# Quarter products for queries, keys and six gates in three interleaved sets

## Chip, cores and metric

The kernel runs on one core of a Trainium2 chip. The metric is device time in microseconds of one launch; the median of three runs is given. The core has TensorE (PE; matmuls, with weight loads shown apart as PEld), VectorE (DVE), ScalarE (ACT), GpSimd (POOL) and SyncE (SP, which here issues the DMAs). Each engine works through its own instructions in order and waits for the others by semaphores.

## The reference, cut to what matters

One decoder layer over 512 positions of width 1024, in float32. After a norm, one large projection `u @ w_in` gives queries, keys and values of three attention groups (six heads of 64 each), the input of a pooling branch, the z, xBC and dt inputs of a state-space (SSD) branch, and three gates of width 1024. Each branch ends in a projection to width 1024, which is multiplied by the sigmoid of its gate; the three are added, projected, and a gated ConvFFN follows.

```python
proj = u @ w_in[i]
q, k, v, pool_in, z, xbc, dt_raw, gate_pre = jnp.split(proj, split_idx, axis=-1)
g = jax.nn.sigmoid(gate_pre + b_gate[i])          # three gates, 1024 wide each
...
o, lse = dilated_group_attention(q[:, :, hs], k[:, :, hs], v[:, :, hs], rel_bias[:, hs], dilation, window // dilation)
xbc = jax.nn.silu(causal_dwconv(xbc, conv_w, conv_b))   # four taps, 1536 channels
```

What matters here: group 1 of the attention needs 384 columns of queries and 384 of keys; the gate of the second branch (pooling) has eight blocks of 128 columns; xBC has twelve.

## The kernel before

**Split precision.** Every large product is three matmul passes over rounded parts: high times high, high times low, low times high (`mm3`). The activations are kept as `uh` and `ul`. Weights are fetched by DMA into `raw`, rounded on ACT into `wh` (`cast`, line 195), and DVE makes the rest, `wl = raw - wh` (`lows`, line 215). `mm3` uses `wl` in the last third of its matmuls.

**Jobs and order.** `program()` yields the weight jobs in order. The main loop goes through them: before the body of job n, `prepare` writes the low part of n+1 and then `then` of n+1 (a sum on weights), puts the cast of n+2 on the list `second`, and fetches n+3. The casts have two halves. `flush()` takes what is on the list: it is called at the beginning of each `step()`, and the main loop calls it before the next job until the list is empty. The first half's call puts the second half on the list. The instructions of PE, ACT, DVE and POOL stay in the order in which the program writes them (`ORDERED`); SP's order is left to the scheduler.

**Side work.** `step()` is called within job bodies. It moves on all generators in `running` and starts one item of `waiting`. An attention item of `attend(g)` writes scores on PE (for every second head), then bias add and maximum on DVE, four exponentials on ACT; two steps later it turns the probabilities on PE, copies them out, and pairs of heads go on to the output product.

**A gate or xBC block** is a "column": 24 matmuls 512 wide into one bank, then an evacuation (gate: sigmoid on ACT, product on DVE; xBC: one ACT instruction, three on DVE) and a `step()`. A job of 256 columns holds two.

**Seven quarter products.** For a pair of blocks (left and right) the product over the even and odd blocks of the contraction and the halves of the positions is made as seven products of a quarter instead of eight. Their sums of activations are made once (`sums_of_u`), their sums of weights on DVE for each set (line 339). `v_pair` does so for the values of groups 1 and 2 (384 columns each; positions as the stationary side), `qk_sevens(1)` for queries and keys of group 1 (384 columns each; 36 matmuls 256 wide for each of seven products). The other products stay whole.

**PSUM** has four banks with tag "mm" (`MM`) and four with tag "sm" (`SM`). Attention items and other side work take "sm" banks, whole products "mm" banks. The raw weights have two buffers, `wh` three, `wl` two, and `ypool` two: these hold the two weight quarters `w` of a set of sevens, later the xBC blocks 0 to 7.

**Order around the change:** second branch's projection, value pair's weights, gates 0 to 3 (`SPLIT` is 4), seven value products, four products of queries and keys, gates 4 and 5, one product, gates 6 and 7, two products, `attend(1)`, twelve xBC columns, `ssd_start`, queries and keys of group 2.

Of the kernel before, what the change touches and what calls it, by code (L numbers as in the profile page):

```python
# [83 lines left out]
def trunk(ctx: ExitStack, tc, out, x, rel_bias, ln1_g, w_in, b_gate, w_a, pool_w, pool_scale, w_b,  # L84
# [235 lines left out]
    def sums_of(f0, f1, ah, al, found):  # L320
# [3 lines left out]
        dve.tensor_tensor(sa[:, LO], f0[:, HI], f1[:, HI], OP.add)  # L324
        dve.tensor_tensor(sa[:, HI], sa[:, LO], f0[:, LO], OP.subtract)
        dve.tensor_tensor(sb[:, LO], f0[:, LO], f0[:, HI], OP.subtract)
        dve.tensor_tensor(sb[:, HI], f1[:, LO], sa[:, HI], OP.subtract)
# [14 lines left out]
    def sevens(quarter, c, side, W, emit):  # L342

        r1, r2, r3, r5 = {}, {}, {}, {}

        def job(j, load, form, use):
            def body(ws):
                wh, wl = ws  # L350
                parts = side(j)
                for i in range(2):
                    ps = MM("pb")
                    o = slice(i * P, (i + 1) * P)
                    mm3(ps[:, :c], lambda k: wh[:, k, :], lambda k: wl[:, k, :],
                        lambda k: parts[k][0][:, o], lambda k: parts[k][1][:, o], range(4), flip=True)
                    use(i, ps[:, :c])
                step()
            new = Job([load] if load is not None else [], 4, c, body)
            new.form = form  # L360
            if load is None:
                new.load = lambda: None
            return new

        def keep(r, name):
            def use(i, ps):
                r[i] = T(name)[:, :c]
                act.copy(r[i], ps)
            return use

        def p5(i, ps):
            keep(r5, "r5")(i, ps)
            dve.tensor_tensor(r2[i], r2[i], ps, OP.add)

        def p6(i, ps):
            dve.tensor_tensor(r1[i], r1[i], ps, OP.add)
            emit(0, 1, i, r1[i], r2[i])

        def p7(i, ps):
            r3[i] = T("r3")[:, :c]  # L380
            dve.tensor_tensor(r3[i], r1[i], ps, OP.add)
            emit(1, 1, i, r3[i], r5[i])

        one = job("A11", quarter(0, 0), None, keep(r1, "r1"))
        two = job("A12", quarter(1, 0), None, lambda i, ps: emit(0, 0, i, r1[i], ps))
        three = job(4, None, lambda: W[1], keep(r2, "r2"))
        one.then = lambda: diff(one.raw, W[0], one.raw)
        three.then = lambda: diff(W[0], W[1], W[0])
# [1367 lines left out]
```

## Time and profile before

| | |
|---|---|
| runs | 1035.77, 1034.72, 1035.15 us (median 1035.15) |
| profiled execution | 1034.7 us, of which 1033.0 us span from first to last instruction |
| TensorE busy | 1022.2 us, mean granted clock 0.998 |
| DVE, ACT, POOL busy | 690.9, 473.3, 149.6 us |
| the changed stretch | about 190 to 371 us of the span |

A row of the groups' view reads: line, engine, operation, out<-in, shapes, count, then total busy us, mean ns of one, then idle time of the engine before them and what ended it. A row of the timeline: start, length in us, engine, line, operation, and in brackets the idle time before it and who ended it. A row of the chain in order of time: start, length, what.

### The profile page before, as it was taken

Reading aid. Unit: us, or ns where it says so; the run is one execution under the profiler, and the core shown is the slowest. Engines: PE = TensorE matmul, PEld = TensorE weight load, DVE = VectorE, ACT = ScalarE, POOL = GpSimd, SP = SyncE. Lnnn points to the kernel's source line nnn. Section 1 sums busy time; section 2 is a strip of 40 time slices with the busy share of each in tenths; the row PEclk is TensorE's granted clock in tenths of the full one; section 3 lists DMA queues with packets and bytes.
Section 4 is the critical chain, followed back from the end, with each engine's and each line's share of the span. In section 5 each row is a group of like instructions: output and inputs, shape, how many; then the busy total and the mean of one; then the engine's idle time right before and its main releaser. Section 6 shows DMA issues by size and latency. Waiting matters only on the chain.

```text
span 1033.0 us, 13348 instructions
## 1 busy us (share of the span) xinstructions
PE 1022.2 (99%) x5312; PEld 863.1 (84%) x5312; DVE 690.9 (67%) x921; ACT 473.3 (46%) x779; POOL 149.6 (14%) x125
## 2 busy tenths in 40 slices
PE   9999999999999999999999999999999999999997
PEld 9998878899888878888888888898888888888885
DVE  5553566687567658766768656766768676666775
ACT  6432554453356364557445324545444443453342
POOL 2770000000000004210152501101111001111120
PEclk9999999999999999999999999999999999999999
DMA  8344312035242244452244525543233324323142
GB/s 289 115 129 138 109 54 75 31 102 172 94 139 84 86 127 116 144 140 67 67 148 152 174 82 204 171 141 121 82 102 124 102 82 163 123 81 122 62 143 82
DMA packets 115997, 122.35 MB, mean 118 GB/s; under 512 B 5315, under 2 KB 98310, under 8 KB 115935
## 3 DMA queue, kind: packets, MB, share of 16 engines
q1 hardware_dynamic: 115343, 120.64, 36.7%
q8 instruction: 42, 0.69, 0.3%
q10 hardware_dynamic: 592, 0.86, 0.3%
q14 instruction: 20, 0.16, 0.1%
HBM read 117.69 MB, written 2.22 MB: 116 GB/s over the span
## 4 chain that ended last, share of the span: by engine, by line
PE 93%; DVE 3%; ACT 2%; DMA 1%; issue 1%; ACTq 0%; SPq 0%; DVEq 0%
PE pa L234 35%; PE pu L234 21%; PE pb L234 10%; PE p L234 10%; PE pqk L234 6%; PE pa L1607 2%; PE ps L751 1%; PE pu L1407 1%; DVE wl L215 1%; PE ppw L234 1%; PE pt L779 1%; PE po L792 1%; PE py L1077 1%; ACT wh L195 1%; DMA xin<-in_x_dram 1%; PE pyo L1084 1%
## 5 line engine op out<-in xcount | busy, mean ns | idle before, releaser
L215 DVE TENSOR_TENSOR wl<-raw,wh 128x2048 fp32r<-128x2048 f32 (+3 forms) x96 | 218.5, 2278 | 46.7 <-ACT wh L195 38.8
L195 ACT CAST wh<-raw 128x1024 fp32r<-128x1024 f32 (+3 forms) x190 | 189.9, 1017 | 54.9 <-DVE raw L339 32.3
L1268 DVE SCALAR_TENSOR_TENSOR hc<-pu,fcol,hc 128x510 f32<-128x510 f32 x88 | 65.8, 748 | 61.0 <-ACT hc L1265 59.4
L234 PE MATMUL pa<-uh,wh 128*128 128x512 f32 x384 | 98.6, 399 | 0.0
L234 PE MATMUL pa<-ul,wh 128*128 128x512 f32 x384 | 94.9, 389 | 0.0
L234 PE MATMUL pa<-uh,wl 128*128 128x512 f32 x384 | 94.9, 389 | 0.0
L234 PEld LDWEIGHTS pa<-ul,wh 128*128 128x128 f32 x384 | 72.1, 188 | 15.2
L234 PEld LDWEIGHTS pa<-uh,wl 128*128 128x128 f32 x384 | 72.1, 188 | 14.9
L234 PE MATMUL pu<-uh,wl 128*128 128x512 f32 (+1 forms) x352 | 83.6, 380 | 0.2 <-DVE wl L215 0.2
L234 PE MATMUL pu<-uh,wh 128*128 128x512 f32 (+1 forms) x352 | 83.6, 379 | 0.0
L234 PE MATMUL pu<-ul,wh 128*128 128x512 f32 (+1 forms) x352 | 83.5, 379 | 0.0
L234 PEld LDWEIGHTS pa<-uh,wh 128*128 128x128 f32 x384 | 70.1, 188 | 14.5 <-issue 0.7
L234 PEld LDWEIGHTS pu<-uh,wl 128*128 128x128 f32 x352 | 64.1, 188 | 13.0 <-DVE wl L215 0.6
L234 PEld LDWEIGHTS pu<-ul,wh 128*128 128x128 f32 x352 | 64.2, 188 | 12.5
L234 PEld LDWEIGHTS pu<-uh,wh 128*128 128x128 f32 x352 | 64.1, 188 | 12.4
L1273 POOL TENSOR_TENSOR hc<-hc 128x512 f32<-128x512 f32 x22 | 30.4, 1383 | 279.2 <-DVE hc L1268 244.2
L1265 ACT ACTIVATE hc<-pu,fcol,fcol 128x512 f32<-128x512 f32 x40 | 31.2, 780 | 82.0 <-PE pu L234 81.7
L1039 POOL TENSOR_TENSOR xd<-xc,dec 128x512 f32<-128x512 f32 x6 | 6.4, 1063 | 331.5 <-DVE xc L1033 312.6
L772 ACT ACTIVATE sb<-sb,both 128x128 f32<-128x128 f32 (+1 forms) x72 | 30.1, 419 | 33.2 <-DVE both L769 23.2
L1166 ACT ACTIVATE sg<-pa,col 128x512 f32<-128x512 f32 x24 | 16.5, 688 | 58.1 <-PE pa L234 51.3
L1270 ACT ACTIVATE hc<-hc 128x512 f32<-128x512 f32 x22 | 13.9, 632 | 42.9 <-DVE hc L1268 42.9
L915 DVE SCALAR_TENSOR_TENSOR xs<-pa,col,xs 128x509 f32<-128x509 f32 (+2 forms) x24 | 18.0, 749 | 16.4 <-ACT xs L911 15.8
(377 smaller groups left out, 1863.1 us busy)
## 6 DMA issues: line engine op xcount, KB each, us to landing
raw<-in_w_in_dram SPq DMA_DIRECT2D x25, 1024.0 KB
raw<-in_ffn_w_up_dram SPq DMA_DIRECT2D x22, 1024.0 KB
raw<-in_ffn_w_down_dram SPq DMA_DIRECT2D x11, 1024.0 KB
raw<-in_w_o_dram SPq DMA_DIRECT2D x8, 1024.0 KB
raw<-in_w_in_dram SPq DMA_DIRECT2D x14, 512.0 KB
raw<-in_w_in_dram SPq DMA_DIRECT2D x8, 768.0 KB
raw<-in_w_b_dram SPq DMA_DIRECT2D x4, 1024.0 KB
al<-ad SPq DMA_DIRECT2D x16, 256.0 KB
```

Of the source, the lines that this page charges most:

```text
L195: act.copy(job.high[:, :, o], job.raw[:, :, o])
L215: (eng or dve).tensor_tensor(l[:, :, o], job.raw[:, :, o], h[:, :, o].bitcast(F32), OP.subtract)
L234: pe.matmul(ps, l, r, start=first and n == 0, stop=last and n == total - 1, skip_group_check=again)
L751: pe.matmul(pss[i][:, o:o + w * P], q[r, n * P:(n + 1) * P], k[r, kb * P:(kb + w) * P], start=True, stop=True)
L772: act.activation(sb[:, off:off + w * P], sb[:, off:off + w * P], AF.Exp, bias=nm[:, n, h:h + 1], accum_out=ls[:, n, h:h + 1])
L915: dve.scalar_tensor_tensor(t[:, sh:], ps[:, :S - sh], col[:, o_cw + 12 * k + m:o_cw + 12 * k + m + 1], t[:, sh:], OP.mult, OP.add)
L1166: act.activation(s, ps, AF.Sigmoid, bias=col[:, o:o + 1])
L1265: act.activation(t, ps, AF.Identity, bias=ff["c1"][:, ff["b"] + m:ff["b"] + m + 1], scale=fw(2, m))
L1268: dve.scalar_tensor_tensor(t[:, sh:], ps[:, :S - sh], fw(k, m), t[:, sh:], OP.mult, OP.add)
L1270: act.activation(t, t, AF.Silu)
L1273: pool.tensor_tensor(a, a, t, OP.mult)
L1607: pe.matmul(first[2 * n + j][:, lo:hi], a[:, k, j * P:(j + 1) * P], b[:, k, lo:hi], start=a is wh and b is uh and k == 0, stop=a is wl and ...
```

## The change

The sets of seven are built by one function, `sevens`, whose weight sums are additions in place on the two held quarters (`plus`); the activation sums change sign to match. `v_pair` keeps its sums in PSUM: one, six, seven and four add up in the same banks X, five and three in Z, and two in Y; X and Z are "sm" banks. In place of `qk_sevens` there are three sets of two blocks on each side (256 columns): Q0 Q1 with K0 K1, Q2 G0 with K2 G1, G2 G3 with G4 G5, where G are gates of the second branch. Each of a set's seven products has 24 matmuls 256 wide, in four "mm" banks held across the three sets. A step follows every second product.

The order changes too: xBC columns 8 and 9 and gates 6 and 7 come ahead of the value products; the 21 products of the sets are interleaved; xBC columns 10 and 11 stand as single columns (jobs of 128 columns, one step) ahead of the last set's seven and four; `attend(1)` is called after the second set's four, with five products and the two single columns still to come; xBC columns 0 to 7 follow.

```diff
@@ -317,14 +317,14 @@
-    def sums_of(f0, f1, ah, al, found):
+    def sums_of(f0, f1, ah, al, found, s=1):
-        dve.tensor_tensor(sa[:, LO], f0[:, HI], f1[:, HI], OP.add)
+        dve.tensor_tensor(sa[:, LO], f0[:, HI], f1[:, HI], OP.add if s > 0 else OP.subtract)
-        dve.tensor_tensor(sb[:, HI], f1[:, LO], sa[:, HI], OP.subtract)
+        dve.tensor_tensor(sb[:, HI], f1[:, LO], sa[:, HI], OP.subtract if s > 0 else OP.add)
...
-    def sevens(quarter, c, side, W, emit):
...
+    SIDES = {"one": "A11", "two": "A12", "three": 4, "four": "A22", "five": 1, "six": 2, "seven": 3}
+
+    def sevens(quarter, c, W, body):
+
+        jobs = {}
+
+        def plus(to, what):
+            dve.tensor_tensor(to, to, what, OP.add)
+
+        def put(name, source=None, w=0):
+            job = jobs[name] = Job(source or [], 4, c,
+                                   lambda ws: body(name, ws, side_u(SIDES[name])))
+            if source is None:
+                job.load = lambda: None
+                job.form = lambda: W[w]
+
+        for name in ("one", "five", "six", "four"):
+            put(name)
+        put("seven", w=1)
+        put("two", quarter(1, 0))
+        put("three", quarter(1, 1))
+
+        def both_():
+            plus(W[0], jobs["three"].raw)
+            plus(W[1], jobs["three"].raw)
+
+        jobs["one"].then = lambda: plus(W[0], W[1])
+        jobs["three"].then = both_
+        jobs["six"].then = lambda: plus(W[0], jobs["two"].raw)
+        return jobs
...
-                           lambda j, h, l: US.__setitem__((j, p), (h, l)))
+                           lambda j, h, l: US.__setitem__((j, p), (h, l)), -1)
...
+        X, Y, Z, r1, r5 = {}, {}, {}, {}, {}
+        banks = {"one": X, "six": X, "seven": X, "four": X, "five": Z, "three": Z, "two": Y}
...
+        def use(name, i, ps):
+            if name == "one":
+                r1[i] = copy(ps, "r1")
+            elif name == "five":
+                r5[i] = copy(ps, "r5")
+            elif name != "three":
+                t, send = out(name in ("seven", "four"), name in ("six", "seven"), i)
+                if name == "two":
+                    dve.tensor_tensor(t, ps, r1[i], OP.add)
+                elif name == "six":
+                    dve.tensor_tensor(t, Z[i][:, :384], copy(ps, "r2"), OP.subtract)
+                elif name == "seven":
+                    dve.tensor_tensor(t, r5[i], copy(ps, "r7"), OP.subtract)
+                else:
+                    act.copy(t, ps)
+                send()
+
+        def body(name, ws, parts):
+            wh, wl = ws
+            bank = banks[name]
+            if name == "one":
+                for i in range(2):
+                    Z[i] = SM("p5")
+                for i in range(2):
+                    X[i] = SM("p1")
+            fresh = name in ("one", "two", "five")
+            for i in range(2):
+                if name == "two":
+                    Y[i] = MM("p2")
+                ps = bank[i][:, :384]
+                o = slice(i * P, (i + 1) * P)
+                mm3(ps, lambda k: wh[:, k, :], lambda k: wl[:, k, :],
+                    lambda k: parts[k][0][:, o], lambda k: parts[k][1][:, o], range(4),
+                    fresh, True, flip=True, again=not fresh)
+                use(name, i, ps)
+            step()
+
+        jobs = sevens(lambda two, h: [quarter(two, h)], 384, W, body)
+        return load, [jobs[n] for n in ("one", "five", "two", "three", "six", "seven", "four")]
 
     def qk_jobs(g):
...
-    def qk_sevens(g):
...
+    def q_sink(g, c):
+        t = QK["q", g, c] = T(f"q{g}")
+        half = lambda hi: grouped(t, g)[:, :, 64 * hi:64 * hi + 64]
+
+        def two(ps, r):
+            dve.scalar_tensor_tensor(half(0), turned_(ps), 0.125, turned_(r), OP.mult, OP.add)
+
...
+    ROLE, turn_of = {}, [0]
+
+    def set_of_sevens(lefts, rights, x, scales=(1.0, 1.0)):
...
+        def bank(which):
+            if not ROLE:
+                for n in ("c", "y", "a", "b"):
+                    ROLE[n] = MM("p")
+            return ROLE[which]
...
+        def use(name, ps):
+            if name in ("two", "six"):
+                for j, (_, make) in enumerate(lefts if name == "two" else rights):
+                    sinks[name == "six", j] = make()
+            if name == "one":
+                copy(ps, "one", scales)
+            elif name == "five":
+                copy(ps, "five")
+            elif name == "two":
+                for j in range(2):
+                    sinks[0, j][0](cut(ps, j), cut(r["one"], j))
+            elif name == "six":
+                t = copy(ps, "r2")
+                for j in range(2):
+                    sinks[1, j](0, cut(bank("b"), j), cut(t, j))
+            elif name == "seven":
+                t = copy(ps, "r7")
+                for j in range(2):
+                    sinks[1, j](1, cut(r["five"], j), cut(t, j))
+            elif name == "four":
+                for j in range(2):
+                    sinks[0, j][1](cut(ps, j))
+
+        def body(name, ws, parts):
+            wh, wl = ws
+            ps = bank(role.get(name, x))
+            fresh = name in ("one", "two", "five")
+            for c in range(2):
+                cs = slice(c * P, (c + 1) * P)
+                mm3(cut(ps, c), lambda k: wh[:, k, cs], lambda k: wl[:, k, cs],
+                    lambda k: parts[k][0], lambda k: parts[k][1], range(4),
+                    fresh and c == 0, True, again=not fresh or c == 1)
+            use(name, ps)
+            turn_of[0] += 1
+            if turn_of[0] % 2 == 0:
+                step()
+
+        return load, sevens(lambda two, h: [src for _, _, src in quarter(two, h)], 256, W, body)
 
     def attend(g):
...
+    def gate_sink(b, m, left):
+        t = T("gr")
+
+        def gate(to, ps):
+            o = o_bg + 8 * b + m
+            act.activation(to, ps, AF.Sigmoid, bias=col[:, o:o + 1])
+
+        def times():
+            dve.tensor_tensor(MG[m], MG[m], t, OP.mult)
+
+        def two(ps, r):
+            dve.tensor_tensor(t[:, LO], ps, r, OP.add)
+            gate(t[:, LO], t[:, LO])
+
+        def four(ps):
+            gate(t[:, HI], ps)
+            times()
+
+        def put(hi, x, y):
+            dve.tensor_tensor(t[:, (LO, HI)[hi]], x, y, OP.subtract)
+            if hi:
+                gate(t, t)
+                times()
+
+        return (two, four) if left else put
+
     def gate_jobs(b, lo=0, hi=8):
         def evac(m, ps):
...
         load, pair = v_pair()
+        Q = lambda i: (C_Q + 384 + i * P, lambda: q_sink(1, i))
+        K = lambda i: (C_K + 384 + i * P, lambda: k_sink(1, i))
+        G = lambda i, left: (C_GATE + D + i * P, lambda: gate_sink(1, i, left))
+        BC = lambda lo, hi, width: jobs_a(w_in, C_XBC + lo * P, hi - lo, uhk, ulk, KD,
+                                          lambda m, ps: xbc_evac(lo + m, ps), width)
+        loads, s = zip(
+            set_of_sevens((Q(0), Q(1)), (K(0), K(1)), "a", (0.125, 0.125)),
+            set_of_sevens((Q(2), G(0, True)), (K(2), G(1, False)), "c", (0.125, 1.0)),
+            set_of_sevens((G(2, True), G(3, True)), (G(4, False), G(5, False)), "a"))
         yield Call(load)
-        yield from gate_jobs(1, 0, SPLIT)
-        load, begun, ended = qk_sevens(1)
+        yield from BC(8, 10, 256)
+        yield from gate_jobs(1, 6, 8)
         for i, job in enumerate(pair):
             yield job
-            if i == 5:
-                yield Call(load)
-        yield from begun
-        yield from gate_jobs(1, SPLIT, SPLIT + 2)
-        yield ended[0]
-        yield from gate_jobs(1, SPLIT + 2)
-        yield from ended[1:]
-        yield Call(lambda: attend(1))
-        yield from jobs_a(w_in, C_XBC, 12, uhk, ulk, KD, xbc_evac)
+            if i in (4, 5):
+                yield Call(loads[i - 4])
+        spare = BC(10, 12, P)
+        for i, n in ((0, "one"), (0, "five"), (0, "two"), (0, "three"), (0, "six"), (1, "one"),
+                     (0, "seven"), (1, "five"), (0, "four"), (1, "three"), (1, "two"), (1, "six"),
+                     (2, "one"), (1, "seven"), (2, "five"), (1, "four"), (2, "three"), (2, "two"),
+                     (2, "six"), (2, "seven"), (2, "four")):
+            if (i, n) == (0, "four"):
+                yield Call(loads[2])
+            if (i, n) in ((2, "seven"), (2, "four")):
+                yield next(spare)
+            yield s[i][n]
+            if (i, n) == (1, "four"):
+                yield Call(lambda: attend(1))
+        yield from BC(0, 8, 256)
         yield Call(ssd_start)
         yield from qk_jobs(2)
         yield Call(lambda: attend(2))

```

172 lines of the change are left out of this document (50 added, 122 removed).

## The prediction

> **What bounds the kernel now.** I read the page first (busy shares, clock), then TensorE's waits, then the stretch the change touches by windows, by the chain in order of time and by queue.
>
> ```profile
> span 1033.0 us, 13348 instructions
> PE 1022.2 (99%) x5312; PEld 863.1 (84%) x5312; DVE 690.9 (67%) x921; ACT 473.3 (46%) x779; POOL 149.6 (14%) x125
> ...
> PEclk9999999999999999999999999999999999999999
> ```
>
> ```profile
> PE p L234 <- DVE wl L215: 0.5, 1, 0.5
> ```
>
> In the second fence the columns are waiter, releaser, total, times, longest. TensorE is busy 1022.2 of 1033.0 us at full clock. So two things count: matmul time removed, and every microsecond in which TensorE is made to wait, because nothing behind it has slack to give that back. In the stretch of the change it waits once today, 0.5 us for a low part (wl). The profiled execution took 1034.7 us (span 1033.0 and 1.7 around it); the median of the runs is 1035.15, 0.45 more. I sum against 1034.7 and add 0.45 at the end. About 0.2% (2.1 us) can be told from no change.
>
> **Matmul time.** The chain in order of time gives both rates.
>
> ```profile
> 253.48 10.91 PE pa L234 x48
> 264.39 4.31 PE p L234 x36
> ```
>
> A gate's matmul 512 wide costs 10.91/48 = 0.227 us, a 256-wide one of a quarter product 4.31/36 = 0.120 us: two of these are 0.240, so splitting loses 5% of a column's price. Before, six gates are 6x24 = 144 wide ones (32.7 us), queries and keys 7x36 = 252 narrow ones (30.2 us). After, three sets of seven products of 24 are 504 narrow ones: 60.3 us. Seven eighths of the gates' work would be 4.1 us less; the narrower form leaves **-2.6 us**. The value pair keeps its 168 matmuls. The old wait of 0.5 us belongs to the handover from the pair to the old products and goes: **-0.5**.
>
> **What the vector and scalar engines get.** A set's product lasts 24x0.120 = 2.9 us (the old: 4.3). Its weights must pass ACT (cast, two halves), then DVE (low part).
>
> ```profile
> L215 DVE TENSOR_TENSOR wl<-raw,wh 128x2048 fp32r<-128x2048 f32 x10 | 22.9, 2286 | 5.7 <-ACT wh L195 5.7
> L195 ACT CAST wh<-raw 128x1024 fp32r<-128x1024 f32 x20 | 20.8, 1042 | 6.2 <-DMA raw<-in_w_in_dram 6.2
> L215 DVE TENSOR_TENSOR wl<-raw,wh 128x1536 fp32r<-128x1536 f32 x7 | 12.3, 1756 | 1.9 <-ACT wh L195 1.8
> L195 ACT CAST wh<-raw 128x768 fp32r<-128x768 f32 x14 | 11.2, 833 | 6.4 <-DVE raw L339 6.2 <-DMA raw<-in_w_in_dram 0.2
> ...
> L339 DVE TENSOR_TENSOR w<-w,w 128x1536 f32<-128x1536 f32 x2 | 3.5, 1754 | 0.0
> ...
> L1168 DVE TENSOR_TENSOR yo<-yo,sg 128x512 f32<-128x512 f32 x5 | 3.5, 690 | 13.4 <-ACT sg L1166 13.4
> L1166 ACT ACTIVATE sg<-pa,col 128x512 f32<-128x512 f32 x5 | 3.5, 690 | 16.3 <-PE pa L234 16.3
> ...
> L707 DVE TENSOR_TENSOR k<-p,r 128x256 f32<-128x256 f32 x3 | 1.8, 615 | 0.2 <-ACT r L706 0.2
> ```
>
> ```profile
> L1176 ACT COPY yo<-pa x8: 582/586/589, 128.5 to 182.0; 128x512 f32<-128x512 f32 x8
> ```
>
> ```profile
> L324 DVE TENSOR_TENSOR sa<-uf x4: 410/415/418, 175.7 to 198.1; 128x256 f32<-128x256 f32 x4
> ```
>
> The tile views give least, median and most. Drawn on to the new sizes, a cast half of 512 elements is 0.62 us, a low part or a plus of 1024 elements 1.23 (by the step from 1536 to 2048). Per set DVE has 7 lows and 4 pluses, 13.5 us, and its evacuations: six of 0.6 for queries and keys (3.6), or for set 2, all gates, six sums of 0.42 and four products of 0.69 (5.3). That is 17 to 19 of 20.1 us: the mean fits. The old pair loses eight value adds on DVE and gains four copies on ACT; xBC columns 8 and 9 and gates 6 and 7 ahead of it put 2x(3x0.75-0.69) = 3.1 us more on DVE beside 21.8 us of matmuls, in-place sums and the reordered banks add nothing there, DMA carries 1.5 MB less of weights: all **zero**, covered by the matmuls; without that cover the 3.1 us would count.
>
> What isn't covered is the order. A cast for the product after next stands on ACT behind the evacuation of the present one, and the low on DVE behind that. From a product's end to its successor's successor there is 2.9 us and, as wl is first used after 8 matmuls, 0.96 more: 3.8 us. Followed through the queues with these durations:
> - Set 0, six: three ends only one product ahead, and its low (1.23) and two pluses (2.5) stand on DVE before the two query sums (1.2) and the low of six. 0.2 + 0.6 + 1.15 + 1.23 + 2.5 + 1.2 + 1.23, less 0.4 that back-to-back instructions overlap, is 7.7 us after two began; the matmuls get there in 6.7: **0.9** lost.
> - Set 1, four: behind seven's copy 0.6, key difference 0.6, gate difference 0.42, sigmoid 0.69, cast 1.15, low 1.23 with handovers 0.3, 5.0 against 3.8: **1.1**. Three more places lose 0.2 to 0.3 (pair's six, set 2's one, set 1's seven): **0.7**.
>
> These 2.7 us could be 0 if all of it ran ahead, or twice that if the sums on one weight tile wait for each other; I take 2.7.
>
> **Attention among the last products.** attend(1) is now called after set 1's four, so its first four items fall on the steps of set 2's two, the first single xBC column, set 2's seven and the second single column. Before, they fell on whole xBC columns. One such step today, on ACT, then on DVE, and a step's scores and transposes on TensorE:
>
> ```profile
> 293.75 0.78 ACT L911 ACTIVATE xs<-pa,col 128x512 f32<-128x512 f32 x1 [3.56 <-PE pa L234]
> 294.43 1.04 ACT L195 CAST wh<-raw 128x1024 fp32r<-128x1024 f32 x1
> 295.48 1.28 ACT L772 ACT_TABLE_LOAD   x1
> 298.23 0.40 ACT L772 ACTIVATE sb<-sb,both 128x128 f32<-128x128 f32 x1 [1.47 <-DVE both L769]
> ...
> 299.69 0.19 ACT L772 ACTIVATION_READ_ACCUMULATOR sb<-sb,both 128x1 f32 x1
> 300.51 0.78 ACT L911 ACTIVATE xs<-pa,col 128x512 f32<-128x512 f32 x1 [0.63 <-PE pa L234]
> 301.19 1.04 ACT L195 CAST wh<-raw 128x1024 fp32r<-128x1024 f32 x1
> ```
>
> ```profile
> 294.56 2.31 DVE L915 SCALAR_TENSOR_TENSOR xs<-pa,col,xs 128x509 f32<-128x509 f32 x3 [2.04 <-ACT xs L911]
> 296.79 0.68 DVE L765 TENSOR_TENSOR sb<-ps,b 128x512 f32<-128x512 f32 x1
> 297.51 0.69 DVE L769 TENSOR_REDUCE both<-sb 128x4 f32<-128x512 f32 x1
> ```
>
> ```profile
> 305.91 1.09 PE ps L751 x16
> 307.00 0.58 PE pt L779 x4
> ```
>
> The reader should see that from the column's end (293.7) to the last exponential (299.8) ACT's queue is held 6.1 us, and that a job's two cast halves stand on either side of it: the first before the exponentials, the second after. Today the second has another 5.5 us column for cover. In the change a single column or a product has one step, so the second half comes behind the exponentials, and the cover is a 2.9 us product:
> - First single column: the item's scores (1.09) end, add and maximum 1.4, exponentials 1.65, half 0.62: 5.1 after two's end, against 1.09 + 2.9 of matmuls, and some 0.2 of handovers: **1.3**.
> - Second single column: 6.1 + 0.6 after the first, against product 2.9, scores 1.09, transposes 0.58, plus handovers: **2.4**.
> - Set 2's four: from the second column's start DVE has its low 1.23, seven's two gates in turn with ACT (0.42 + 0.69 + 0.69, twice), add and maximum 1.4, then exponentials 1.65, half 0.62, low 1.23: 9.7; the matmuls reach the first wl in 5.45 + 0.58 + 0.96 = 7.0: **2.7**.
> - First whole xBC column: by the order of allocation its bank is the one that four has just filled, and four's two sigmoids stand on ACT behind the second column's 0.7 + 2.31 on DVE, add and maximum, exponentials, a copy 0.56, a cast half 1.04 and a table change 1.28. From four's low to the bank's release 8.5 us, of which four's rest of 16 matmuls covers 1.9: **6.6**. With another bank only wl is late: 3.4.
>
> Sigmoids and exponentials now alternate: five table changes for one today. Most fall into waits; the one before four's gates doesn't, and is priced above by its row.
>
> ```profile
> 364.53 1.04 ACT L195 CAST wh<-raw 128x1024 fp32r<-128x1024 f32 x1
> 365.59 1.28 ACT L1096 ACT_TABLE_LOAD   x1
> 366.88 1.16 ACT L1096 ACTIVATE xcv<-xcv 128x512 f32<-128x512 f32 x2
> ```
>
> Here the load starts as the cast ends and the next activation starts as the load ends: 1.28 us in all. [...]
>
> The sum: -2.6 - 0.5 + 2.7 + (1.3 + 2.4 + 2.7 + 6.6 = 13.0) = **+12.6 us**, 1047.3 for the profiled execution, **1047.8** on the scale of the median. The same with the cheaper bank and small product waits: 1042; with doubled ones: 1051.
>
> **The rivals.**
> 1. *Faster.* ACT and DVE run a product ahead all through, so no cast or low is late, and only -3.1 is left: 1032.1. It decides when all new waits together stay below 1.0 us.
>
> ```profile
> 279.60:288.30 8.70, 8.70 (x74) 8.67 (x73) 6.57 (x6) 5.27 (x10) 0.00 (x0) 1.00 0.39 122
> ```
>
> For it: in this window (stretch, length, then busy time and count of PE, PEld, DVE, ACT, POOL) two old products keep TensorE busy throughout, with DVE at 76%. Against: such a job lasts 4.3 us and takes two steps. Chance 0.13.
> 2. *About the same.* The second cast halves get ahead of the exponentials, so the 13.0 shrinks to 1.6 (four's low and bank without attention, 0.5 + 1.1): -3.1 + 2.7 + 1.6 = +1.2, 1036.3. The three ACT rows 294.43 to 301.19 speak against it: order is kept. Chance 0.10.
> 3. *Late weights.* The pair's value rows go out by SP.
>
> ```profile
> 235.94 10.54 SPq L624 DMA_DIRECT2D vr<-v  x16
> 246.59 46.33 SPq L183 DMA_DIRECT2D raw<-in_w_in_dram  x8
> ```
>
> ```profile
> 251.72 2.00 ACT L195 CAST wh<-raw 128x1024 fp32r<-128x1024 f32 x2 [5.73 <-DMA raw<-in_w_in_dram]
> ```
>
> If two's weights of set 0 stand behind sixteen sends (10.5 us) and land 5.1 us after issue, two starts up to 6.9 us late: up to 1054.7. For it: at 251.72 ACT waited 5.73 us for exactly that. Against: its slot is free long before. Chance 0.07.
> 4. *Slower clock.* [...] Chance 0.06. [...]
>
> That the change saves no matmuls can be left out: the counts are in the code.
>
> **How the numbers follow.** The forecast has 0.64. Faster by over 0.2% is rival 1: 0.13; within 0.2% rival 2: 0.10; slower the rest, 0.77. The range leaves out rival 1 and the end of rival 3: 1036 to 1053.
>
> **What would show it.** In the changed profile: 5420 matmuls, TensorE's busy time of narrow matmuls 60 us, five table loads between the first set and the second whole xBC column, TensorE's waits led by ACT (gr, the first whole column's bank) and by wh and wl around the single columns, 10 to 17 us in all, and no wait downstream changed. It is wrong if these waits add to under 5 us, or if exponentials come behind both halves of a cast.

## The result: 1046.4 us against 1035.3, slower by 1.1%, and the profile after

The changed kernel takes 1046.42 us (median; 1045.84 to 1047.41), the kernel before 1035.3 (four runs now, 1034.72 to 1035.77); the ratio is 1.0109 with an interval of 1.0091 to 1.0126. The prediction said 1047.8. Sign, size and place are as predicted. Inside the sum the terms at attention were too large, and a wait that was to go came back in the same place; that the total comes so close is in part luck.

The page of the changed kernel, in the parts that answer to those shown of before:

```profile
span 1044.1 us, 13664 instructions
...
PE 1024.6 (98%) x5420; PEld 868.4 (83%) x5420; DVE 703.5 (67%) x942; ACT 490.1 (47%) x815; POOL 148.9 (14%) x125
```

TensorE has 2.4 us more of busy time and, with the longer span, 8.7 us more of idle. The matmuls are fewer in work but more in number (5420). Its waits (waiter, releaser: total, times, longest):

```profile
PE pa L234 <- ACT wh L195: 3.4, 2, 2.2
PE pa L234 <- DVE wl L215: 3.1, 1, 3.1
PE p L234 <- DVE wl L215: 2.9, 4, 1.1
PE pa L1648 <- DVE relb L497: 1.1, 1, 1.1
PE pcb L1051 <- ACT xcv L1139: 1.0, 1, 1.0
```

The last two rows stood in before as well. The first three are new: 9.4 us, of which 6.5 lie at whole columns (pa) and 2.9 at quarter products (p). Before there was one such row, 0.5 us. By windows, the stretch falls apart as follows (stretch, length, busy time and count of PE, PEld, DVE, ACT, POOL, then TensorE's granted clock, DMA share, GB/s):

```profile
206.30:235.80 29.50, 29.45 (x169) 29.10 (x168) 21.80 (x20) 14.74 (x24) 0.00 (x0) 1.00 0.32 99
235.80:291.40 55.60, 53.55 (x433) 52.15 (x432) 42.73 (x44) 27.73 (x54) 0.00 (x0) 1.00 0.34 100
291.40:331.00 39.60, 31.90 (x197) 26.81 (x198) 23.15 (x32) 26.32 (x60) 0.00 (x0) 0.96 0.26 79
```

The pair (first row) is nearly gapless. 18 quarter products (second row) idle 2.1 us. The stretch with attention and the two single columns (third row) idles 7.7 us of 39.6, and its clock is 0.96. TensorE's own rows there show each place, with the idle time and its cause in brackets:

```profile
240.32 0.74 PE L234 MATMUL p<-sah,wl 128*128 128x256 f32 x4 [0.53 <-DVE wl L215]
249.94 0.74 PE L234 MATMUL p<-sah,wl 128*128 128x256 f32 x4 [0.72 <-DVE wl L215]
283.55 0.74 PE L234 MATMUL p<-uh,wl 128*128 128x256 f32 x4 [0.56 <-DVE wl L215]
296.91 2.11 PE L234 MATMUL pa<-uh,wh 128*128 128x512 f32 x8 [1.27 <-ACT wh L195]
309.37 3.51 PE L234 MATMUL pa<-uh,wh 128*128 128x512 f32 x8 [2.18 <-ACT wh L195]
319.22 0.74 PE L234 MATMUL p<-uh,wl 128*128 128x256 f32 x4 [1.12 <-DVE wl L215]
321.24 2.00 PE L234 MATMUL pa<-uh,wh 128*128 128x512 f32 x8
328.19 2.14 PE L234 MATMUL pa<-uh,wl 128*128 128x512 f32 x8 [3.14 <-DVE wl L215]
```

In order: set 0's five, set 0's six, set 1's four, the first single column, the second single column, set 2's four, and the first whole column, which starts without a wait at 321.24 and then stands 3.14 us at its low part. ACT's rows before the second single column give the reason, the same as in the prediction's rows of before:

```profile
303.36 0.61 ACT L195 CAST wh<-raw 128x512 fp32r<-128x512 f32 x1
307.17 0.40 ACT L815 ACTIVATE sb<-sb,both 128x128 f32<-128x128 f32 x1 [3.19 <-DVE both L812]
...
308.72 0.60 ACT L195 CAST wh<-raw 128x512 fp32r<-128x512 f32 x1
```

The first half of the column's cast is done at 303.97. ACT then waits 3.19 us for the item's maximum, does the exponentials, and only then the second half (308.72), for which TensorE has been waiting since 307.2. At the first whole column the order is the same, one step later: the second half of its cast stands behind the item's exponentials (322.75 to 324.40) and a copy, and DVE's low part behind that. It ends at 328.14, and TensorE goes on at 328.19.

```profile
324.78 1.04 ACT L195 CAST wh<-raw 128x1024 fp32r<-128x1024 f32 x1
325.85 2.29 DVE L215 TENSOR_TENSOR wl<-raw,wh 128x2048 fp32r<-128x2048 f32 x1 [3.13 <-ACT wh L195]
```

### The profile page after: what moved, and what is told of

Read it like the earlier page. It is cut to its first block, busy times and chain, and to the rows that moved or that the text cites. A ratio compares the mean times of both kernels' runs of the same rounds, so it can differ in the third digit from the quotient of the medians.

```text
span 1044.1 us, 13664 instructions
## 1 busy us (share of the span) xinstructions
PE 1024.6 (98%) x5420; PEld 868.4 (83%) x5420; DVE 703.5 (67%) x942; ACT 490.1 (47%) x815; POOL 148.9 (14%) x125
## 4 chain that ended last, share of the span: by engine, by line
PE 89%; DVE 5%; ACT 3%; DMA 1%; issue 1%; SPq 0%; ACTq 0%; DVEq 0%
PE pa L234 31%; PE pu L234 22%; PE p L234 12%; PE pb L234 8%; PE pqk L234 6%; PE pa L1691 2%; DVE wl L215 1%; PE pu L1476 1%; PE ppw L234 1%; PE ps L794 1%; PE po L835 1%; PE pt L822 1%; DMA w<-in_w_in_dram 1%; ACT wh L195 1%; PE py L1120 1%
## 5 line engine op out<-in xcount | busy, mean ns | idle before, releaser
L215 DVE TENSOR_TENSOR wl<-raw,wh 128x2048 fp32r<-128x2048 f32 (+3 forms) x94 | 208.7, 2222 | 56.2 <-ACT wh L195 48.7
L195 ACT CAST wh<-raw 128x1024 fp32r<-128x1024 f32 (+3 forms) x186 | 180.8, 993 | 44.1 <-DVE raw L339 26.1
L234 PE MATMUL pa<-uh,wh 128*128 128x512 f32 x336 | 88.0, 405 | 3.4 <-ACT wh L195 3.4
L234 PE MATMUL pa<-uh,wl 128*128 128x512 f32 x336 | 83.2, 390 | 3.1 <-DVE wl L215 3.1
L234 PE MATMUL pa<-ul,wh 128*128 128x512 f32 x336 | 83.3, 390 | 0.0
L234 PEld LDWEIGHTS pa<-uh,wl 128*128 128x128 f32 x336 | 63.0, 188 | 16.6 <-DVE wl L215 3.6
L234 PEld LDWEIGHTS pa<-uh,wh 128*128 128x128 f32 x336 | 62.1, 191 | 16.9 <-ACT wh L195 4.1
L234 PEld LDWEIGHTS pa<-ul,wh 128*128 128x128 f32 x336 | 63.4, 189 | 13.5
L234 PEld LDWEIGHTS pu<-uh,wh 128*128 128x128 f32 x352 | 64.1, 188 | 12.4
L215 DVE TENSOR_TENSOR wl<-w,wh 128x1024 fp32r<-128x1024 f32 (+2 forms) x25 | 38.5, 1540 | 9.4 <-ACT wh L195 9.4
L195 ACT CAST wh<-w 128x512 fp32r<-128x512 f32 (+2 forms) x50 | 35.4, 747 | 16.0 <-DVE w L349 10.6
```

The lines of the kernel that those rows point to most:

```text
L195: act.copy(job.high[:, :, o], job.raw[:, :, o])
L215: (eng or dve).tensor_tensor(l[:, :, o], job.raw[:, :, o], h[:, :, o].bitcast(F32), OP.subtract)
L234: pe.matmul(ps, l, r, start=first and n == 0, stop=last and n == total - 1, skip_group_check=again)
```

## The experiments

The theory (A in the texts on record): the 11 us are the order on ACT and DVE around attention's items, which hold casts and bank evacuations behind them where the next job is short. Rivals: the products' weight traffic by itself; table changes; late fetches.

**1. Attention after the products.** The call moves behind the loop over the 21 products; nothing else changes.

```diff
-            if (i, n) == (1, "four"):
-                yield Call(lambda: attend(1))
+        yield Call(lambda: attend(1))
```

> attend(1) is called after the last of the 21 products instead of after the second set's four; the work is the same. Theory A (order: attention items on ACT and DVE among short products and single columns): the waits at the two single columns (1.3 and 2.2 us), at set 2's four (1.1, about 0.5 stays), at the first whole column (3.1) and the 1.6 us that the second single column ran at half clock go, so about 9 us less than the changed kernel: 1037.5 us, within 1 to 3 us of the kernel before. Theory B (the short products themselves overload ACT and DVE, wherever attention stands): the items only meet other work later, at most 3 us less, above 1043.

Measured: 1034.65 us, 11.8 less than the changed kernel, where theory A expected about 9 and theory B at most 3; against before 0.9993 (0.9984 to 1.0002). Its span is 1033.4 us, 10.7 less than the changed kernel's. The only waits that it has in the stretch:

```profile
PE p L234 <- DVE wl L215: 2.1, 4, 0.7
```

All waits at whole columns are gone, and with them the one at L1051. The 10.7 us add up: 7.5 of waits (1.27, 2.18 and 3.14 at the columns, and the 1.12 at set 2's four shrinks to 0.26), 1.7 of slower clock at the second single column, 1.0 at L1051, and the rest restarts after the waits (a group of four narrow matmuls that had to wait takes 0.74 us, the others 0.64). So the loss is the place of one call, and what the products lose by themselves just eats what they save. The 1.0 at L1051 is no loss of the change, though, as the kernel before has that wait too (its L1008).

**2. Casts in one piece.** The casts of 1024 elements aren't halved, so no second half stands behind the exponentials.

```diff
+        cuts = 1 if job.k * job.c == 1024 else cuts
```

> The casts of jobs of 1024 weights per partition (the sets' products and the single columns) are one ACT instruction instead of two halves, so that no half stands behind an item's exponentials. If the place of the second half were all, the waits at the single columns, four and the first whole column would all go: 9 us less, 1037. If the queues of ACT and DVE also carry too much there (theory A as followed through the queues), the waits at the two single columns and the half clock go (5 us) but four and the first whole column start earlier and wait 1.5 to 2 us more: about 3 us less, 1043. Theory B: no change.

Measured: 1044.45, ratio 1.0086 (1.0071 to 1.0101); 2.0 less than the changed kernel, not 3 (four runs each, 1043.45 to 1045.50 against 1045.84 to 1047.41). The waits moved:

```profile
PE pa L235 <- DVE wl L216: 2.6, 1, 2.6
PE p L235 <- DVE wl L216: 2.3, 2, 1.6
PE p L235 <- ACT wh L196: 2.0, 3, 1.0
```

The wait at the single columns for wh is gone, but quarter products now wait for wh, and the whole column's low is nearly as late as in the changed kernel (2.6 for 3.1). The halving of the cast is where the delay showed, not what made it: whatever ACT does next stands behind the exponentials.

**3. No weight sums.** The twelve sums in place of the three sets are left out, so that the products use the quarters as they were fetched; the pair keeps its sums.

```diff
-            dve.tensor_tensor(to, to, what, OP.add)
+            if c == 384:
+                dve.tensor_tensor(to, to, what, OP.add)
```

> The four sums on weights of each of the three sets are left out (the products then use the held quarters as they are); the value pair keeps its own. Theory A: only the small waits among the products shrink (about 3 us to 1) and the end of the sets stays as it is: 1.5 to 2.5 us less than the changed kernel, 1044.5. Theory B: 14.7 us less work on DVE empties the queue, and most of the 11 us go: below 1039.

Measured: 1044.89, ratio 1.009 (1.0075 to 1.0105): 1.5 less (1044.81 to 1044.99 against 1045.84 to 1047.41).

```profile
PE pa L234 <- ACT wh L195: 3.4, 2, 2.2
PE pa L234 <- DVE wl L215: 3.2, 1, 3.2
PE p L234 <- DVE wl L215: 1.6, 2, 1.1
```

The products' waits fall from 2.9 to 1.6, those at the columns don't move. DVE's load is a small part of the loss, and none of that at attention.

**4. No sigmoid.** The gates of the sets use the identity in place of the sigmoid, which leaves out the table changes among the last products.

```diff
-            act.activation(to, ps, AF.Sigmoid, bias=col[:, o:o + 1])
+            act.activation(to, ps, AF.Identity, bias=col[:, o:o + 1])
```

> The sigmoids of the six gates in the sets become the plain sum with bias (no table needed), so the table changes among the last products fall from five to one. By the rows a change costs 1.28 us of ACT and three of the four lie in time that ACT spends waiting: 0 to 0.7 us less, 1046. [...]

Measured: 1046.92, ratio 1.0104 (1.0087 to 1.0121), the same as the changed kernel. Between 285 and 331 us of its span ACT loads a table once, not four times, and TensorE's waits stay:

```profile
PE pa L234 <- ACT wh L195: 3.4, 2, 2.2
PE pa L234 <- DVE wl L215: 3.2, 1, 3.2
PE p L234 <- DVE wl L215: 2.7, 4, 0.9
```

The three loads that are gone weren't on the path by more than the runs' spread (1045.12 to 1047.35). The load that stays is the first, at the first single column, and on that one the run says nothing.

**5. The pair alone.** The kernel before with the changed value pair and its sums of activations; queries and keys of group 1 stay as before and get one sum with the other sign.

```diff
-    def sevens(quarter, c, side, W, emit):
+    def sevens(quarter, c, W, body):
...
-                           lambda j, h, l: US.__setitem__((j, p), (h, l)))
+                           lambda j, h, l: US.__setitem__((j, p), (h, l)), -1)
...
-        return load, sevens(quarter, 384, side_u, W, emit)
+        jobs = sevens(lambda two, h: [quarter(two, h)], 384, W, body)
+        return load, [jobs[n] for n in ("one", "five", "two", "three", "six", "seven", "four")]
```

> The kernel before with one part of the change: the value pair adds up in banks and its weight sums are additions in place; queries, keys, gates and the order stay as before. (The old products of queries and keys then meet activation sums of the other sign, so those come out changed; the work is the same.) Theory A: the pair takes 0.3 us longer as in the changed trace, and the handover wait of 0.5 us after it shrinks: within 0.5 us of before, 1035.3. Rival: the pair is where the change gains, at least 1.5 us faster, 1033.5.

Measured: 1035.34, ratio 0.9997 (0.9987 to 1.0006). The pair costs and gains nothing clear of the spread. But at the handover to the old products, where TensorE waited 0.5 us before, it waits 1.3 us (at 242.51, for wl), where a smaller wait was expected, and inside the pair its six waits 0.2 us (at 224.35).

**6. Later sums on GpSimd**, on top of experiment 1: of the four sums in place of each set, and of the pair, the two that are needed later leave DVE for GpSimd, which is idle there.

```diff
+        def plus(to, what, eng=dve):
+            eng.tensor_tensor(to, to, what, OP.add)
...
-            plus(W[1], jobs["three"].raw)
+            plus(W[1], jobs["three"].raw, pool)
...
-        jobs["six"].then = lambda: plus(W[0], jobs["two"].raw)
+        jobs["six"].then = lambda: plus(W[0], jobs["two"].raw, pool)
```

> As attention_later, and two of each set's four weight sums (the one for seven, the one for four) are made by GpSimd, which is idle there. The 21 products take 4.5 us longer than their matmuls in attention_later. If DVE's queue of sums is the cause of a quarter of it (six of set 0, the small waits): 1 us less than attention_later, 1033.6. If GpSimd's slower additions (1.3 us for 512 elements in the trace before) delay seven and four instead, or disturb DVE: no less, up to 1 us more.

Measured: 1045.09, ratio 1.0089 (1.0074 to 1.0104). Against experiment 1 a gain of 1 was expected, 10.4 were lost.

```profile
PE p L234 <- DVE wl L215: 8.6, 7, 2.1
```

In experiment 1 these waits were 2.1 us. Two waits for wh, 1.5 us, are new as well, and for 3.4 us from 245.92 the clock is at half. The timeline shows the cause at one of the places:

```profile
242.75 2.37 POOL L349 TENSOR_TENSOR w<-w,raw 128x1024 f32<-128x1024 f32 x1 [11.88 <-DMA vr<-v]
243.74 2.47 DVE L215 TENSOR_TENSOR wl<-w,wh 128x1024 fp32r<-128x1024 f32 x1 [1.21 <-ACT wh L195]
```

GpSimd takes 2.37 us for the sum, and the low part that DVE does beside it takes 2.47 instead of 1.23. So for this sum DVE gains nothing by giving it away, and the low part is late; TensorE's wait for it is 1.81 us.

**7 and 8. The same with a column ahead, and with casts in one piece.** Experiment 7 adds to 6: column 10 between the pair and the sets, and a job of columns 0 and 1 ahead of set 2's four; experiment 8 adds the edit of experiment 2 to 6.

```diff
         spare = BC(10, 12, P)
+        yield next(spare)
...
+            if (i, n) == (2, "four"):
+                yield from BC(0, 2, 256)
...
```

> As later_sums_on_gpsimd, with the single xBC column 10 between the value pair and the sets instead of ahead of set 2's seven (column 11 goes there, and columns 0 and 1 as one job ahead of its four). The wait of set 0's five for its weights (0.7 us; they land 5.5 us after the pair's sends) should be covered by the column: 0.7 us less than later_sums_on_gpsimd, 1032.9. Rival: the column's own three DVE instructions (2.3 us) push the wait to the next products: the same as without.

> As later_sums_on_gpsimd, with the casts of products and single columns in one ACT instruction (1.04 us for two of 0.6). Through the queues: 0.2 to 0.5 us less, 1033.3, if ACT's chain of evacuation and cast is what is late at four of set 1; unchanged if DVE is.

Measured: 1048.69, ratio 1.0121 (1.0106 to 1.0136), and 1044.87, ratio 1.0084 (1.0069 to 1.0099). Experiment 7 costs 3.6 us more than 6, where 0.7 less or nothing was expected. The waits at its products are alike (9.6 us, against 10.1); what grew is the time at half clock (13.7 us, against 3.4; the mean granted clock is 0.992, against 0.997) and a wait of 2.0 us at L1051. Experiment 8 is 0.2 less, within the spread. Neither undoes what GpSimd costs; experiment 9 asks for the column without GpSimd.

**9. A column ahead of the sets**, on top of experiment 1, without GpSimd.

```diff
         spare = BC(10, 12, P)
+        yield next(spare)
...
-            if (i, n) in ((2, "seven"), (2, "four")):
+            if (i, n) == (2, "seven"):
                 yield next(spare)
```

> Attention items called after the 21 products, and xBC column 10 moved from ahead of set 2's seven to between the value pair and set 0's one. Theory A (in the later-attention order, 1034.65, what is left are the products' own waits for wl: 2.1 us as 0.56 at set 0's five, 0.72 at set 0's six, 0.56 at set 1's four and a 0.3; a column ahead of set 0 gives five's weights 5.5 us more): the first of these goes, and the set starts a full column ahead, so six's shrinks too; 1033.5 to 1034.2. Rival (what is left is the rate of the vector and scalar engines over three sets, so a start ahead is used up by set 1): no change, 1034.6, or, as two columns no longer stand in the last set, 0.5 us more there.

Measured: 1040.61, ratio 1.005 (1.0037 to 1.0062): 6 us lost where up to 1.1 was expected as gain. Both theories missed.

```profile
252.03 0.74 PE L234 MATMUL p<-sbh,wh 128*128 128x256 f32 x4 [0.87 <-ACT wh L195]
258.29 0.74 PE L234 MATMUL p<-sah,wl 128*128 128x256 f32 x4 [1.34 <-DVE wl L215]
316.43 2.12 PE L234 MATMUL pa<-uh,wh 128*128 128x512 f32 x8 [1.51 <-ACT wh L195]
```

```profile
242.22 5.30 SPq L601 DMA_DIRECT2D vr<-v  x8
247.62 12.83 SPq L183 DMA_DIRECT2D raw<-in_w_in_dram  x5
251.36 1.14 ACT L195 CAST wh<-raw 128x512 fp32r<-128x512 f32 x2 [2.44 <-DMA raw<-in_w_in_dram]
```

The column takes one of the two raw buffers. The fetch for set 0's three, which in experiment 1 goes out at 227.77, stands behind the pair's last eight value rows here (242.22), and ACT waits 2.44 us for it; three, six and their sums are late one after the other. At the end, where no column stands ahead of set 2's four any more, TensorE waits 1.51 us at the first whole column, where experiment 1 has no wait.

**10. The same with three's sums parted**: only the sum that six needs stays ahead of six's low part.

```diff
         def both_():
-            plus(W[0], jobs["three"].raw)
             plus(W[1], jobs["three"].raw)
+            plus(W[0], jobs["two"].raw)
...
-        jobs["three"].then = both_
-        jobs["six"].then = lambda: plus(W[0], jobs["two"].raw)
+        jobs["three"].then = lambda: plus(W[0], jobs["three"].raw)
+        jobs["six"].then = both_
```

> As the run with column 10 ahead, and three's two sums in place are parted: only the one that six needs stays ahead of six's low part, the other goes behind it (behind three's and six's low parts and with the sum of two). Theory A (order on the vector engine, not its total, makes six late: one plus of 1.23 us fewer stands ahead of six's low): set 0's wait at six, 0.72, goes; 0.5 to 0.9 us less than the run beside it, unless seven's cast, which waits for the moved sum, comes late in its place. Rival (the engine's mean load, 17 to 19 of 20.1 us a set, leaves no room wherever the sum stands): within 0.2 us of the run beside it, the wait moved to seven or four.

Measured: 1044.64, ratio 1.009 (1.0077 to 1.0104), 4 us more than experiment 9, where at best 0.9 less was expected.

```profile
PE pa L234 <- ACT wh L195: 3.3, 2, 1.8
PE p L234 <- DVE wl L215: 3.3, 7, 0.6
PE p L234 <- ACT wh L195: 1.4, 1, 1.4
```

Six's wait does shrink (1.34 to 0.48), as the first theory said, but there are three short waits more, three's cast is later still (1.4), and the single column, which had no wait, stands 1.80 us for wh and then runs at half clock for 3.4 us.

**11. Two columns in one job**, attention where the change puts it: columns 10 and 11 as a job of 256 columns ahead of set 2's seven.

```diff
-        spare = BC(10, 12, P)
...
-            if (i, n) in ((2, "seven"), (2, "four")):
-                yield next(spare)
+            if (i, n) == (2, "seven"):
+                yield from BC(10, 12, 256)
```

> The changed kernel with attention where the change puts it, but xBC columns 10 and 11 as one job of 256 columns ahead of set 2's seven, in place of one column ahead of seven and one ahead of four. Theory A (a cast half or low part behind an attention step's exponentials needs a 5.5 us column behind it for cover; a 2.9 us product isn't enough): the wait at column 10 stays (1.3), that between the columns goes, and the steps of column 11 and seven still hit seven and four; of the 7.7 us of waits around the single columns about half stays, 1041 to 1044. Rival (what counts is the number of attention steps before the whole columns, not what stands behind each): 1046 as the changed kernel, since the steps are as many.

Measured: 1045.55, ratio 1.01 (1.0085 to 1.0116). That is nearer to the rival's 1046 than to the theory's 1041 to 1044, and not clear of the changed kernel's spread (1044.06 to 1045.93 against 1045.84 to 1047.41).

```profile
314.95 1.03 PE L234 MATMUL p<-uh,wh 128*128 128x256 f32 x4 [2.29 <-ACT r L726]
326.45 2.11 PE L234 MATMUL pa<-uh,wl 128*128 128x512 f32 x8 [2.79 <-DVE wl L215]
```

Between the two columns nothing waits any more, as the theory said. But four now waits 2.29 us for its bank, which ACT's copy (r) empties only after the exponentials. So it is not enough to give the cast cover: with each step ACT is held by an item, and the next short product finds either its weights or its bank late.

**12. Attention after the products, and an earlier fetch.** On top of experiment 1, set 0's held quarters are fetched after the pair's two, not after its six.

```diff
-            if i in (4, 5):
-                yield Call(loads[i - 4])
+            if i in (2, 5):
+                yield Call(loads[i == 5])
```

> As the run with attention after the 21 products (1034.65), with the two fetches of set 0's held quarters called after the pair's two instead of after its six, so that on SP they stand ahead of the value rows of six and seven. Theory A (in that run set 0's one and its sum wait for these fetches, 1.10 us on ACT and 1.02 on DVE, and so five's low is 0.57 late): five's wait of 0.57 goes, and some of six's 0.72 with it; 0.5 to 1.0 us less, 1033.6 to 1034.2, DVE's wait on w gone. Rival (buffer: the set's quarters wait for a buffer that comes free only late in the pair, so the fetch holds up SP and the pair's sends): no gain or some 0.5 us lost, with SP waiting at the fetch.

Measured: 1034.02, ratio to before 0.9985 (0.9976 to 0.9994): faster than both kernels, by 1.4 us than before and by 12.4 than the change. Of the 1.4 us, 1.0 is the wait at L1051, which the kernel before has and this one hasn't. Experiment 1 is 0.6 us slower, as expected, but the intervals of the two overlap. Its span is 1031.9 us, and its waits in the stretch are:

```profile
PE p L234 <- DVE wl L215: 1.6, 3, 0.7
```

Five's wait (0.57) is gone, six's (0.75) isn't. ACT's and DVE's waits for the fetch shrank from 1.10 and 1.02 us to 0.63 and 0.33; they aren't gone.

## Why the prediction was right, step by step

**Matmul time, -2.6: borne out.** There are 5420 matmuls, and away from waits their starts are 0.120 us apart (in the changed kernel's timeline twelve from 285.08 to 286.52). The 60 us can't be read from the groups' busy time, where pipelined records overlap (groups of four last 0.64 us and start 0.48 apart); 504 times the distance gives 60.5. Experiment 12 bears it out: with -2.6, the old wait (-0.5), 3.8 that its pair and products lose by their starts, and two waits that only the kernel before has (1.0 at its L1008, 0.5 at its L1624) the sum is -0.8; its span is 1.1 us shorter than that of the kernel before.

**The old handover wait, -0.5: this step failed.** The wait stood at the second product behind the pair, and there, at set 0's five, the changed kernel has one of the same size (240.32, 0.53):

```profile
241.23 0.74 PE L234 MATMUL p<-sah,wl 128*128 128x256 f32 x4 [0.46 <-DVE wl L215]
```

This is the row of the kernel before. In the change five's weights come late because the fetch of a held quarter stands behind value rows on SP (it goes out at 231.22, and DVE's sum at 236.55 has waited 1.09 us for it): a small form of rival 3. Experiment 12 fetched earlier, and the wait went. That the wait of before has the same cause is not shown.

**The products' waits, +2.7: right where places were named.** The 18 products up to set 2's two take 55.60 us; 432 times 0.120 is 51.8, so 3.8 are lost. Only 1.8 of that stands in brackets (0.53, 0.72, 0.56). The rest shows in the starts: groups of four are 0.48 us apart, and a group that had to wait takes 0.1 more. Counted so, six of set 0 loses 1.0 (0.9 predicted) and four of set 1 1.15 (1.1). The three more places are there as well, without a bracket: the low parts of set 2's one (273.38), set 1's seven (276.63) and the pair's six (224.59) start 0.21, 0.27 and 0.22 late, each 0.05 us after DVE's wl has ended; with the restarts that is 1.0 (0.7 predicted). What the prediction's sum lacks is five, 0.8. With the pair's six, which lies ahead of the 18 products, the term is 4.1.

**Attention, +13.0: 10.6.** These are the five places, from the starts of TensorE's groups:

| place | predicted | measured | how |
|---|---|---|---|
| first single column | 1.3 | 1.5 | wait 1.27 |
| second single column | 2.4 | 2.4 | wait 2.18, the rest around it |
| its clock | 0 | 1.7 | 7.19 us for a column of 5.47 (as in experiment 1) |
| set 2's four | 2.7 | 1.5 | wait 1.12, 4.33 us for 2.87 |
| first whole column | 6.6 | 3.5 | wait 3.14, 9.02 us for 5.5 |
| sum | 13.0 | 10.6 | |

The first two terms are right to 0.2 us, and the second half does stand behind the exponentials (296.25 and 308.72). The first is right for another reason in part. Its own terms (1.09, 1.4, 1.65, 0.62) make 4.8 and not 5.1, and a table load stands in it that the prediction let fall into a wait:

```profile
293.40 1.28 ACT L815 ACT_TABLE_LOAD   x1
294.70 0.40 ACT L815 ACTIVATE sb<-sb,both 128x128 f32<-128x128 f32 x1
```

The item's maximum is ready at 294.02 (DVE's row of 293.33, 0.69 us long), so the load holds the exponentials back by some 0.6 us. That is read from the rows; no run leaves this load out.

The step that failed most is the bank: the prediction took it from the order of allocation that the whole column's bank is the one four has just filled. The row at 321.24 starts the column's first eight matmuls at once after four, while four's bank is read by its sigmoids only at 327.13; so the column has another bank, and it was free. Only wl was late, the alternative priced at 3.4; 6.6 became 3.5. Four's 2.7 was too much because the second column before it took 1.7 us longer, while DVE and ACT went on: four's wl ends 9.8 us after that column's start, 9.7 were predicted, but the matmuls get there later. It is part of the same delay, counted where the clock fell. With the products' 4.1, and 0.5 less for the wait at L1624, which the changed kernel hasn't, the measured terms make -2.6 - 0.5 + 4.1 + 10.6 - 0.5 = 11.1; the spans differ by 11.1. The forecast was 1.5 us above that because 3.1 too much for the bank and 1.2 for four outweighed the clock (1.7) and five (0.8), which were not in the sum: there the closeness is luck.

**Table loads: five, as predicted (293.40, 309.83, 314.19, 325.83, 334.23).** The one before four's gates was priced at 1.28 on the path; experiment 4 removed it and two more and won nothing, as nothing waited for four's bank. Each stands for 1.28 us, and the next ACT instruction starts at its end (that at 325.83 is followed at 327.13) or, after those of 314.19 and 334.23, waits 0.27 and 0.24 us more for DVE.

**What would show it.** The new waits are 9.4 us, just under the 10 to 17 foreseen, and the rest of the loss is the slower clock, restarts, and late starts without a bracket. They are led by wh and wl, as foreseen, but none is for gr or for a bank.

**The rivals.** Rivals 1 and 2 needed the casts ahead of the exponentials; they came behind. Rival 3 shows in small. Rival 4, the slower clock, is what the prediction took too lightly: in the changed kernel the clock fell to 0.50 after a wait of 2.18 us and not after the one of 3.14, for 3.41 us, and that cost 1.7. No run shows a whole column at half clock, from which the upper end of the range, 1053, was worked out.

What experiments 2 and 11 add is a correction to the theory itself. The prediction told the loss as a cast's half that lacks cover. Taking away the halving (2) or giving cover (11) returned 2.0 and 0.9 us (the latter not clear of the spread), where 3 and 2.4 to 5.4 were expected; moving the items (1) returned 11.8. The loss is that items and short products share ACT in order; where it shows is only where it is seen first.

## What to carry to other kernels

Price side work by what it holds back on the engine that feeds the next job, and call it where jobs are long: one call moved behind the products was worth 11.8 us, more than all else that was tried. Removing the wait that the profile names (a cast's half, a sum ahead of a low part) moved the loss on more often than not; when the releaser's queue is full up to the item, move the item. Before a job is put ahead as cover, look at the buffers it takes and at whose fetches that pushes behind what on SP.

## What the hardware showed that was not expected

**Half clock did not go by the length of the wait before it.** In the changed kernel TensorE's granted clock is 0.50 for 3.41 us from 309.71, behind the wait of 2.18 us at the second single column, and stays at 1.00 behind the wait of 3.14 us at the first whole one (stretch, length, busy time of PE and so on, with the clock as third number from the end):

```profile
306.30:309.71 3.41, 1.23 (x12) 0.83 (x9) 1.15 (x3) 2.54 (x10) 0.00 (x0) 1.00 0.00 0
309.71:313.12 3.41, 3.41 (x10) 2.67 (x9) 2.23 (x4) 2.29 (x4) 0.00 (x0) 0.50 0.41 105
...
323.36:326.78 3.42, 1.70 (x8) 1.08 (x6) 0.93 (x1) 3.40 (x9) 0.00 (x0) 1.00 0.00 0
326.78:330.19 3.41, 2.00 (x8) 1.42 (x8) 2.87 (x4) 3.06 (x5) 0.00 (x0) 1.00 0.23 56
```

In the 3.41 us ahead of the fall TensorE idles 64% of its time. In the two stretches of this length around the longer wait it idles 50% and 41%. In experiment 4 a wait of 3.15 us at the same place is followed by matmuls at half the rate, four in 2.08 us where the changed kernel has eight in 2.14 (328.19):

```profile
328.38 2.08 PE L234 MATMUL pa<-uh,wl 128*128 128x512 f32 x4 [3.15 <-DVE wl L215]
```

Half clock came with waits of 2.29 (experiment 11), 1.81 (6) and 1.80 us (10), but not with those of 2.79 (11), 2.07 (6) and 1.51 (9); with a wait of 1.74 us it came in experiment 7 and not in 6. What decides is not shown. The fall at the second single column cost 1.7 us (7.19 us for a column of 5.47), about as much as the changed kernel's four executions differ (1045.84 to 1047.41 us, with mean clocks of 0.995 to 0.997).

**DVE took longer beside GpSimd's additions** (experiment 6): 2.47 us for 1.23 at a low part (243.74), and 3.31 for 1.23 at a sum in place (257.50, beside GpSimd's sum from 256.41, 3.32 us long). So here the idle GpSimd was no free place for the sums beside a busy DVE.
